# Block encoder on one core: Strassen-Winograd products of the feed-forward chained in the PSUM banks

## The chip, the cores and the metric

The kernel runs on one core of a Trainium2 chip. The metric is the device time of one execution in microseconds (us), from runs of the whole program; TensorE's matmul queue is PE, its weight loads are PEld, VectorE is DVE, ScalarE is ACT, GpSimd is POOL, and SP is the queue that issues all the transfers of the kernel.

## The reference, cut to what matters

One encoder layer on 1024 tokens of width 1024: attention and a pooling mixer with an output projection, and then a SwiGLU feed-forward of inner width 2816, all in float32.

```python
h = rmsnorm(x, norm2_g)
x = x + (jax.nn.silu(h @ w_gate) * (h @ w_up)) @ w_down
```

## The kernel before, in words

Every float32 operand is split into a high part in fp32r and the rest ("hi" and "lo"), and every product of two 128-row pieces is three matmuls with 512 columns: hi·hi, hi·lo, lo·hi (`PASSES`). A split costs two instructions: a copy or cast for hi (ACT, DVE or POOL), and one subtraction for lo (DVE or POOL, `combine`, line 337).

The front half (projections, pooling, attention, output projection, up to about 440 us) is not touched. What follows is the feed-forward:

- Four plain tiles each for the first gate and up block (`plain_tile`), while the sums T1 to T4 of the normed activations are made (`sums_of`).
- Twenty blocks, ten of gate and ten of up in turn (`block`). A block makes 256 inner channels for all 1024 tokens as a 2 x 2 product in the Strassen-Winograd form: seven products of 12 matmuls. Its left operands are A11, A12, A22 and the sums S1 = A21 + A22, S2 = S1 - A11, S3 = A11 - A21, S4 = A12 - S2 of the weights. The right ones are B11, B21, B22 and T1 to T4. The products are P1 = A11·B11, P2 = A12·B21, P3 = S4·B22, P4 = A22·T4, P5 = S1·T1, P6 = S2·T2, P7 = S3·T3, and with U2 = P1 + P6 and U3 = U2 + P7 the four parts of the result are C11 = P1 + P2, C12 = U2 + P5 + P3, C21 = U3 - P4, C22 = U3 + P5.
- After every second pair of gate and up a down stage (`down_sums`, five in all): the same form with activations on the left and rows of `w_down` on the right, for two pairs at once (index i = 0, 1) and four row tiles t. Each of the seven names is 2 x 4 x 3 = 24 matmuls into four banks, 168 in a stage. `drain` adds the banks to the residual rows `qp`.
- A last, plain down product (`down`) and the stores.

In `block` before, every product has a bank of its own (`any_bank`, eight banks in two pools). DVE or ACT reads each bank once or more: P1 is copied to `u` on ACT, P6, P5, P7 are added to sums `u` and `x` in SBUF on DVE (`added`, line 1297), and `emit` adds a bank to a sum on DVE (lines 1252 and 1269), applies SiLU on ACT (line 1258), or multiplies on DVE (line 1272). In `drain` a bank goes straight into `qp` (line 1384) or through sums: two of four rows keep U2 in SBUF and add it to `qp` from there on DVE or POOL, the other two keep it in the bank and take P6 and P7 in through a copy `temp` on ACT.

The order of the work is made by a planner (`Flow`) when the program is built: every vector instruction has a cost, jobs have ranks from the deadline that TensorE sets them, and each engine gets one fixed queue. `flow.tensor(cost, ...)` moves the planner's clock on by the cost of three matmuls. `K["down"]` holds a surcharge per product name that sends work from DVE to POOL in the down stage. Operands are prepared up to two products ahead (`AHEAD = 2`) in three `ring` buffers; right operands of the down stage go to three `raw` buffers or to `wk` slots.

Of the kernel before, what the change touches and what calls it, by code (L numbers as in the profile page):

```python
# [18 lines left out]
P = 128  # L19
# [23 lines left out]
NSLOT = 33  # L43
# [9 lines left out]
    "down": [1.35, 1.05, 1.25, 1.25, 0.75, 1.65, 0.95], "wide": 2,  # L53
# [219 lines left out]
def block_kernel(  # L273
# [667 lines left out]
    def open_silu():  # L941
        late["half"] = sb(ctx, "half", bufs=8, side="right")
        late["sums"] = work()
# [120 lines left out]
    DOWN = ("A11", "A12", "S1", "S2", "S3", "S4", "A22")  # L1064
    STEADY = ("A11", "S1", "A12", "S2", "S3", "S4", "A22")
# [3 lines left out]
    for b in range(len(blocks)):  # L1069
        stream += [(b, name) for name in (FIRST if b < 2 else STEADY)]  # L1070
        if b % 4 == 3:
            stream += [((b // 2 - 1, b // 2), name, i) for name in DOWN for i in range(2)]
# [66 lines left out]
    def product(bank_, w, name, start=True, stop=True):  # L1139
        for i in range(PARTS):  # L1140
            x, job = moving(name, i)
            flow.tensor(0.649, w[1], job)
            for j, (a, b) in enumerate(PASSES):
                nc.tensor.matmul(bank_, w[0][:, a, i], x[:, b], start=(start and i == 0 and j == 0), stop=(stop and i == PARTS - 1 and j == 2))  # L1144

    silu, gated, g_raw, g_job, users = {}, {}, {}, {}, []
# [19 lines left out]
    def sums(p, name):  # L1166
# [22 lines left out]
        elif name == "S4":  # L1189
            job = go(a(0, 1), a(0, 1), a(1, 0), ALU.subtract, made["S2"], made["split A12"])  # L1190
# [7 lines left out]
        elif name == "T4":  # L1198
            job = go(b(1, 0), b(0, 1), b(1, 0), ALU.subtract, made["T2"], made["split B21"])
# [5 lines left out]
    def make_pair(p, name):  # L1205
# [3 lines left out]
        left = {"A11": (0, 0), "S1": (1, 0), "A12": (0, 1), "S2": (1, 0), "S3": (0, 0), "S4": (0, 1), "A22": (1, 1)}[name]  # L1209
# [8 lines left out]
        if name == "S4" or (name == "A22" and p % 2 == 1):  # L1218
            y = pieces()
            waits_r += [made["split T3"], made["T4"]]  # L1220
# [10 lines left out]
        if name == "S2":  # L1231
            sums(p, "S3")
            sums(p, "S4")
            sums(p, "T4")
            sums(p, "T3")
        return (x, jl), (y, jr)

    def emit(b, q, psum, name, plus, *waits):

        kind, p = blocks[b]  # L1240
        f, h = 2 * p + int(q[0]) - 1, int(q[1]) - 1
        if kind == "g":
            s = late["half"].tile([P, HALF], F32, tag="half", name="silu")

            def first():
                yield list(waits)
                if plus is None:
                    yield act(512)
                    nc.scalar.activation(s, psum, AF.Silu)
                else:  # L1250
                    yield dve(512)
# [414 lines left out]
```

## Time and profile before

| | |
|---|---|
| runs (3), median | 1125.41 us (1124.94 to 1126.28) |
| profiled execution, its own time | 1121.88 us |
| its span, first to last instruction | 1120.1 us |
| mean granted TensorE clock, share of 2.4 GHz | 0.994 |
| PE busy | 1074.5 us, 96% of the span |
| DVE, POOL, ACT busy | 871.0, 555.6, 455.8 us |

The time of an execution is its span and 1.8 us around it. Busy time of an engine holds what an instruction waited inside it; idle time in front of an instruction is given with what ended it. Starts are in us from the start of the span.

### The profile page before, as it was taken

How to read it: one execution, taken by the hardware profiler on the slowest of the kernel's cores; microseconds unless marked ns; L12 is line 12 of the kernel's file. 1: busy time of each engine (PE TensorE's matmuls, PEld its weight loads, DVE VectorE, ACT ScalarE, POOL GpSimd, SP SyncE). 2: the span in 40 equal slices, each digit the busy share in tenths (PEclk: the TensorE clock that was granted, in tenths of full speed). 3: DMA queues.
4: the chain of work that ended last, by engine and by line, in shares of the span. 5: the costliest groups of instructions: out<-in, count | busy, mean ns of one | idle time of the engine just before them, and what ended most of it. 6: DMA issues, size and time to landing. Idle time of an engine off the chain costs nothing.

```text
span 1120.1 us, 14036 instructions
## 1 busy us (share of the span) xinstructions
PE 1074.5 (96%) x5114; PEld 877.6 (78%) x5114; DVE 871.0 (78%) x1371; ACT 455.8 (41%) x810; POOL 555.6 (50%) x454
## 2 busy tenths in 40 slices
PE   6989988999999999999999999999899999999998
PEld 5967876888888888878778877888688867887787
DVE  7886699976676776787997689767976698668985
ACT  6513367666676654622332233222422232223420
POOL 3182575533334214664863388236843486238820
PEclk9999999999999999999999999999999999999999
DMA  7111111000000101030123002210122012200113
GB/s 264 53 36 60 37 57 38 19 20 13 16 20 10 30 29 50 27 119 14 36 66 106 19 0 95 61 71 1 38 94 94 1 38 77 94 19 4 53 57 151
DMA packets 42565, 58.49 MB, mean 52 GB/s; under 512 B 4224, under 2 KB 32768, under 8 KB 42496
## 3 DMA queue, kind: packets, MB, share of 16 engines
q1 hardware_dynamic: 42496, 57.59, 15.9%
q8 instruction: 40, 0.66, 0.2%
q14 instruction: 29, 0.24, 0.1%
HBM read 53.39 MB, written 4.19 MB: 51 GB/s over the span
## 4 chain that ended last, share of the span: by engine, by line
PE 72%; DVE 14%; POOL 4%; issue 3%; ACT 1%; DMA 0%; DVEq 0%; ACTq 0%; POOLq 0%
PE b L1144 35%; PE b L1417 8%; PE b L890 8%; PE b L853 5%; PE b L840 5%; PE b L810 5%; DVE wk L337 2%; POOL wk L337 2%; DVE silu L337 2%; DVE qp L1384 2%; PE b L1369 2%; PE b L583 2%; DVE ring L337 1%; DVE wk L1297 1%; DVE qp L337 1%
## 5 line engine op out<-in xcount | busy, mean ns | idle before, releaser
L1144 PE MATMUL b<-wk,ring 128*128 128x512 f32 x1872 | 427.1, 389 | 1.8 <-DVE ring L324 1.8
L1144 PEld LDWEIGHTS b<-wk,ring 128*128 128x128 f32 x1872 | 350.8, 188 | 76.6 <-DVE ring L324 2.3
L1417 PE MATMUL b<-raw,ring 128*128 128x512 f32 x660 | 158.6, 394 | 8.8 <-POOL raw L337 3.6
L1417 PEld LDWEIGHTS b<-raw,ring 128*128 128x128 f32 x660 | 121.9, 188 | 43.8 <-POOL raw L337 8.4
L337 POOL TENSOR_TENSOR ring<-raw,ring 128x512 fp32r<-128x512 f32 x59 | 78.1, 1324 | 150.4 <-ACT ring L322 123.6
L829 POOL TENSOR_SCALAR wk<-wk,rsm 128x1024 f32<-128x1024 f32 x64 | 74.7, 1174 | 141.4 <-ACT wk L821 76.9
L322 ACT ACTIVATE ring<-raw 128x512 fp32r<-128x512 f32 x85 | 52.9, 630 | 206.7 <-PE b L1144 92.4
L331 DVE TENSOR_TENSOR wk<-b,wk 128x512 fp32r<-128x512 f32 (+1 forms) x160 | 101.5, 658 | 37.7 <-ACT wk L322 37.6
L322 ACT ACTIVATE wk<-b 128x512 fp32r<-128x512 f32 (+1 forms) x160 | 90.1, 576 | 80.3 <-PE b L840 60.4
L1384 DVE TENSOR_TENSOR qp<-qp,b 128x512 f32<-128x512 f32 (+1 forms) x167 | 105.6, 675 | 12.4 <-PE b L1369 9.0
L337 DVE TENSOR_TENSOR ring<-raw,ring 128x512 fp32r<-128x512 f32 x91 | 78.4, 867 | 44.3 <-POOL ring L326 22.2
L890 PE MATMUL b<-wk 128*128 128x512 f32 x384 | 102.3, 396 | 0.0
L337 POOL TENSOR_TENSOR wk<-wk 128x512 f32<-128x512 f32 (+3 forms) x55 | 78.4, 1439 | 26.1 <-ACT wk L322 14.8
L810 PE MATMUL b<-kT,wk 128*128 128x512 f32 x256 | 89.1, 430 | 0.0
L853 PE MATMUL b<-wk,vv 128*128 128x512 f32 x256 | 81.8, 398 | 4.7 <-DVE wk L331 4.5
L322 ACT ACTIVATE ring<-silu 128x512 fp32r<-128x512 f32 x65 | 40.9, 629 | 109.6 <-PE b L1417 32.3
L890 PEld LDWEIGHTS b<-wk 128*128 128x128 f32 x384 | 70.8, 188 | 15.2
L819 DVE TENSOR_REDUCE nm<-b 128x1 f32<-128x1024 f32 x64 | 77.9, 1217 | 3.8 <-PE b L810 2.6
L821 ACT ACTIVATE wk<-b,nm 128x1024 f32<-128x1024 f32 x64 | 71.4, 1115 | 18.9 <-DVE nm L819 18.5
L337 POOL TENSOR_TENSOR ring<-silu,ring 128x512 fp32r<-128x512 f32 x45 | 60.5, 1344 | 36.4 <-ACT ring L322 36.4
L840 PE MATMUL b<-ident,wk 128*128 128x128 f32 x512 | 76.7, 272 | 0.7 <-POOL wk L829 0.7
L840 PEld LDWEIGHTS b<-ident,wk 128*128 128x128 f32 x512 | 63.5, 140 | 17.5 <-POOL wk L829 0.9
(145 smaller groups left out, 1590.8 us busy)
## 6 DMA issues: line engine op xcount, KB each, us to landing
raw<-in_w_gate_dram SPq DMA_DIRECT2D x22, 512.0 KB, 3.7
raw<-in_w_up_dram SPq DMA_DIRECT2D x22, 512.0 KB, 3.8
wk<-in_w_down_dram SPq DMA_DIRECT2D x20, 512.0 KB, 5.2
raw<-in_w_in_dram SPq DMA_DIRECT2D x10, 512.0 KB, 3.8
qp<-in_x_dram SPq DMA_DIRECT2D x8, 512.0 KB, 8.0
raw<-in_w_out_dram SPq DMA_DIRECT2D x8, 512.0 KB, 3.4
out_dram<-qp SPq DMA_DIRECT2D x15, 256.0 KB, 2.0
raw<-in_x_dram SPq DMA_DIRECT2D x14, 256.0 KB, 2.7
```

The source lines that it names most:

```text
L322: nc.scalar.activation(hi, src, AF.Copy)
L331: nc.vector.tensor_tensor(lo, src, hi.bitcast(F32), op=ALU.subtract)
L337: (nc.gpsimd if way[0] == "G" else nc.vector).tensor_tensor(dst, a, b, op=op)
L810: nc.tensor.matmul(s[:, c * 512:(c + 1) * 512], qT[t][0][:, h * P:(h + 1) * P], kT[:, kv, b, c * 512:(c + 1) * 512], start=(b == 0), stop= ...
L819: nc.vector.tensor_reduce(nm, s, axis=AX, op=ALU.max, negate=True)
L829: nc.gpsimd.tensor_scalar(pe, pe, rs, 1.0, op0=ALU.mult, op1=ALU.mult)
L840: nc.tensor.transpose(pt[:, j * P:(j + 1) * P], pe[:, c * P:(c + 1) * P], ident)
L853: nc.tensor.matmul(po[t, kv], vt, ps[:, b], start=(c == 0 and b == 0), stop=(c == NT - 1 and b == 1))
L890: nc.tensor.matmul(self.py, mix[self.t][a][:, k, :], wo[k][b][:, self.cs], start=(self.i == 0 and i == 0), stop=(self.i == NK - 1 and i == 2))
L1144: nc.tensor.matmul(bank_, w[0][:, a, i], x[:, b], start=(start and i == 0 and j == 0), stop=(stop and i == PARTS - 1 and j == 2))
L1384: nc.vector.tensor_tensor(dst, dst, src, op=op)
L1417: nc.tensor.matmul(banks[t][0], x[:, a, t * P:(t + 1) * P], y[:, b], start=(i == 0 and j == 0), stop=(i == 1 and j == 2))
```

## The change

Three banks serve the seven products of a block. P1, P6, P7 and P4 follow each other in one bank, so that it holds P1, then U2, then U3, then C21 (the sign of T4 is turned round for this). P5 and P3 follow each other in a second bank, P2 has a third. Each state that is needed is read between two products; before TensorE adds the next product to a bank it waits for the reading, and a whole product in another bank lies between. The order of the names becomes A11, S1, S2, S4, S3, A12, A22. The down stage does the same with four banks for A11, S2, S3, A22, four for S1, S4, and four again for A12, and every state goes straight from the bank into its block of `qp`: `drain` is gone. Three `wk` slots more are paid for by a smaller descriptor scratch. The planner's cost of three matmuls goes from 0.649 or 0.648 to 0.68, and `K["down"]` becomes 0.9 throughout.

```diff
-NSLOT = 33
+NSLOT = 36
+SCRATCH = 4096
...
-    "down": [1.35, 1.05, 1.25, 1.25, 0.75, 1.65, 0.95], "wide": 2,
+    "down": [0.9] * 7, "wide": 2,
...
-    DOWN = ("A11", "A12", "S1", "S2", "S3", "S4", "A22")
-    STEADY = ("A11", "S1", "A12", "S2", "S3", "S4", "A22")
+    STEADY = ("A11", "S1", "S2", "S4", "S3", "A12", "A22")
...
-            flow.tensor(0.649, w[1], job)
+            flow.tensor(0.68, w[1], job, *(waits if i == 0 else ()))
...
-            job = go(a(0, 1), a(0, 1), a(1, 0), ALU.subtract, made["S2"], made["split A12"])
+            job = go(a(1, 0), a(0, 1), a(1, 0), ALU.subtract, made["S3"], made["split S2"], g_job[2 * p + 1, 0])
...
-            job = go(b(1, 0), b(0, 1), b(1, 0), ALU.subtract, made["T2"], made["split B21"])
+            job = go(b(1, 0), b(1, 0), b(0, 1), ALU.subtract, made["T2"], made["split B21"])
...
+        py, held = any_bank()
+        product(py, operand("A11"), "B11")
+        j = copied(u, py, *of_u)
+        pz, held_z = any_bank()
+        product(pz, operand("S1"), "T1")
+        jz = copied(v, pz, *of_v)
+        product(py, operand("S2"), "T2", start=False, more=True, waits=[j])
+        jx = copied(x, py, *of_x)
+        product(pz, operand("S4"), "B22", start=False, more=True, waits=[jz])
...
+        product(py, operand("S3"), "T3", start=False, more=True, waits=[jx])
...
+        pw, held_w = any_bank()
+        product(pw, operand("A12"), "B21")
...
+        product(py, operand("A22"), "T4", start=False, more=True, waits=[j2])
...
+        BANKS = {"S2": "A11", "S4": "S1", "S3": "A11", "A22": "A11"}
+        INTO = {"A11": (0, 0), "S1": (NR, 1), "S2": (0, 1), "S4": (0, 1), "S3": (NR, 1), "A12": (0, 0), "A22": (NR, 0)}
+        for k, name in enumerate(STEADY):
...
+                    waits = [read[own, t]] if i == 0 and own != name else []
+                    flow.tensor(0.68, jx, jy, *waits)
...
+                        row, c = INTO[name]
+                        job = read[own, t] = into(row + t, c, psum)
```

Where instructions stand now. First ACT, in a gate block and the up block behind it (`b1`, `b3` are banks; `silu`, `wk_4535`, `wk_4536` take the states; `ring` is a left operand's hi). Before:

```order
L1290 ACTIVATE wk_4535<-b3_5600 128x512
L322 ACTIVATE ring_5625<-raw_5451 128x512
L322 ACTIVATE ring_5666<-raw_5451 128x512
L1258 ACTIVATE silu_5664<-silu_5664 128x512
L322 ACTIVATE ring_5708<-raw_5601 128x512
L1258 ACTIVATE silu_5704<-silu_5704 128x512
L1258 ACTIVATE silu_5726<-silu_5726 128x512
L322 ACTIVATE ring_5728<-raw_5601 128x512
L1258 ACTIVATE silu_5745<-silu_5745 128x512
L1290 ACTIVATE wk_4535<-b1_5746 128x512
```

And now:

```order
L1310 ACTIVATE silu_5556<-b3_5580 128x512
L1310 ACTIVATE silu_5557<-b3_5558 128x512
L1258 ACTIVATE silu_5557<-silu_5557 128x512
L1258 ACTIVATE silu_5556<-silu_5556 128x512
L323 ACTIVATE ring_5673<-raw_5559 128x512
L1258 ACTIVATE silu_5555<-silu_5555 128x512
L1258 ACTIVATE silu_5690<-b3_5558 128x512
L323 ACTIVATE ring_5694<-raw_5559 128x512
L1310 ACTIVATE wk_4535<-b1_5691 128x512
L1310 ACTIVATE wk_4535<-b1_5712 128x512
L323 ACTIVATE ring_5730<-raw_5559 128x512
L1310 ACTIVATE wk_4536<-b1_5691 128x512
```

Three bank copies per block stand on ACT where one stood (the first of this gate block is the row ahead of these), and the last SiLU of a gate block reads its bank.

Second, POOL at the start of a steady down stage (`silu` holds the gated values and their sums, `wk` rows of `w_down` and their sums, `ring` and `raw` the split left and right operands). Before:

```order
L326 TENSOR_SCALAR ring_7045<-silu_6636 128x512
L326 TENSOR_SCALAR raw_7046<-wk_6576 128x512
L337 TENSOR_TENSOR ring_7045<-silu_6636,ring_7045 128x512
L337 TENSOR_TENSOR raw_7046<-wk_6576,raw_7046 128x512
L337 TENSOR_TENSOR silu_6891<-silu_6891,silu_6869 128x512
L337 TENSOR_TENSOR ring_7091<-silu_6617,ring_7091 128x512
L337 TENSOR_TENSOR raw_7092<-wk_6536,raw_7092 128x512
L337 TENSOR_TENSOR raw_7117<-wk_6812,raw_7117 128x512
L337 TENSOR_TENSOR silu_6617<-silu_6617,silu_6555 128x512
L337 TENSOR_TENSOR wk_6536<-wk_6576,wk_6536 128x512
```

And now:

```order
L327 TENSOR_SCALAR ring_6909<-silu_6385 128x512
L327 TENSOR_SCALAR raw_6910<-wk_6426 128x512
L338 TENSOR_TENSOR ring_6909<-silu_6385,ring_6909 128x512
L338 TENSOR_TENSOR raw_6910<-wk_6426,raw_6910 128x512
L338 TENSOR_TENSOR wk_6426<-wk_6482,wk_6426 128x512
L338 TENSOR_TENSOR silu_6385<-silu_6385,silu_6383 128x512
L338 TENSOR_TENSOR wk_6689<-wk_6744,wk_6689 128x512
L338 TENSOR_TENSOR ring_6953<-silu_6385,ring_6953 128x512
L338 TENSOR_TENSOR silu_6647<-silu_6647,silu_6645 128x512
L338 TENSOR_TENSOR ring_6978<-silu_6647,ring_6978 128x512
L338 TENSOR_TENSOR wk_7025<-wk_6744,wk_7025 128x512
```

The two split operands in front are A12's before and S1's now, and the sums T2 (`wk_6426`) and S2 (`silu_6385`) of the first pair stand four and three places earlier. From the first to the last down matmul POOL's queue holds 18 subtractions and additions and 6 TENSOR_SCALAR; the queue of DVE holds 22 instructions of line 338 there, and 28 bank readings belong to the stage.

Third, DVE in the same stage, from the splits of S2's right operand on. Before, behind the readings of three products:

```order
L337 TENSOR_TENSOR silu_6555<-silu_6595,silu_6617 128x512
L337 TENSOR_TENSOR ring_7136<-silu_6617,ring_7136 128x512
L337 TENSOR_TENSOR wk_6536<-wk_6536 128x512
L1384 TENSOR_TENSOR qp_84<-qp_84,b3_7138 128x512 x2
L1384 TENSOR_TENSOR qp_84<-qp_84,b3_7143 128x512 x2
L1384 TENSOR_TENSOR qp_84<-qp_84,b1_7150 128x512 x2
L337 TENSOR_TENSOR ring_7161<-silu_6891,ring_7161 128x512
L1384 TENSOR_TENSOR qp_84<-qp_84,b3_7154 128x512 x2
```

And now, behind the readings of one product:

```order
L338 TENSOR_TENSOR wk_6426<-wk_6426 128x512
L338 TENSOR_TENSOR raw_6954<-wk_6426,raw_6954 128x512
L338 TENSOR_TENSOR silu_6383<-silu_6384,silu_6385 128x512
L1414 TENSOR_TENSOR qp_84<-qp_84,b1_6955 128x512
L1414 TENSOR_TENSOR qp_84<-qp_84,b3_6960 128x512
L338 TENSOR_TENSOR raw_6979<-wk_6689,raw_6979 128x512
L338 TENSOR_TENSOR silu_6385<-silu_6518,silu_6385 128x512
L1414 TENSOR_TENSOR qp_84<-qp_84,b1_6966 128x512
L338 TENSOR_TENSOR wk_7001<-wk_6482,wk_7001 128x512
L338 TENSOR_TENSOR silu_6645<-silu_6646,silu_6647 128x512
L338 TENSOR_TENSOR ring_7000<-silu_6385,ring_7000 128x512
L338 TENSOR_TENSOR silu_6647<-silu_6780,silu_6647 128x512
```

A bank of S1 was read twice and is read once; the operands of S2 (`raw_6954`, `raw_6979`) and of S4 (`wk_7001`, `ring_7000`) and the sums S3 and S4 stand between its four readings.

## Rows read from the trace of the kernel before

**Rows 1.** Page, busy time, share of the span and instructions by engine.
```profile
PE 1074.5 (96%) x5114; PEld 877.6 (78%) x5114; DVE 871.0 (78%) x1371; ACT 455.8 (41%) x810; POOL 555.6 (50%) x454
```
**Rows 2.** Chain that ended last, in time: start, us, engine, tile, count; down stages one, four, five.
```profile
529.72 9.53 PE b L1417 x42
...
574.00 76.16 PE b L1144 x336
...
890.96 9.54 PE b L1417 x42
...
936.78 76.16 PE b L1144 x336
...
1012.94 9.53 PE b L1417 x42
...
1057.17 38.08 PE b L1144 x168
```
**Rows 3.** Windows, two pairs of blocks and the down stage behind: busy us by engine, instructions.
```profile
573.84:650.00 76.16, 76.16 (x337) 63.06 (x336) 54.53 (x81) 18.91 (x31) 27.95 (x23) 1.00 0.20 66
650.00:694.23 44.23, 40.43 (x170) 30.95 (x168) 40.72 (x52) 17.00 (x29) 38.97 (x29) 1.00 0.11 30
```
**Rows 4.** Timeline of PE, second down stage: start, us, instructions, idle before and what ended it.
```profile
667.42 1.45 PE L1417 MATMUL b<-raw,ring 128*128 128x512 f32 x5 [0.71 <-POOL raw L337]
...
672.17 8.41 PE L1417 MATMUL b<-raw,ring 128*128 128x512 f32 x34 [0.41 <-DVE ring L337]
...
682.95 0.97 PE L1417 MATMUL b<-wk,ring 128*128 128x512 f32 x3 [0.56 <-DVE wk L1297]
685.24 3.71 PE L1417 MATMUL b<-wk,ring 128*128 128x512 f32 x15 [1.33 <-DVE wk L1297]
```
**Rows 5.** Groups of DVE by form, 650.00 to 694.23: busy, mean ns, idle before.
```profile
L1384 DVE TENSOR_TENSOR qp<-qp,b 128x512 f32<-128x512 f32 x24 | 15.1, 678 | 0.5 <-PE b L1417 0.4
...
L1297 DVE TENSOR_TENSOR b<-b,temp 128x512 f32<-128x512 f32 x4 | 2.8, 690 | 0.1
L1297 DVE TENSOR_TENSOR wk<-b,wk 128x512 f32<-128x512 f32 x4 | 2.6, 680 | 0.1
...
L1272 DVE TENSOR_TENSOR silu<-b,silu 128x512 f32<-128x512 f32 x2 | 1.4, 687 | 0.0
...
L1269 DVE TENSOR_TENSOR b<-b,wk 128x512 f32<-128x512 f32 x1 | 0.7, 699 | 0.1
```
**Rows 6.** Groups of POOL by form, the same stretch, the two TENSOR_SCALAR.
```profile
L326 POOL TENSOR_SCALAR ring<-silu 128x512 fp32r<-128x512 f32 x1 | 0.6, 625 | 2.2 <-PE b L1144 2.2
L326 POOL TENSOR_SCALAR raw<-wk 128x512 fp32r<-128x512 f32 x1 | 0.6, 620 | 0.0
```
**Rows 7.** Timeline of POOL, then of DVE, in the same stage.
```profile
651.43 1.29 POOL L337 TENSOR_TENSOR ring<-silu,ring 128x512 fp32r<-128x512 f32 x1
652.68 1.29 POOL L337 TENSOR_TENSOR raw<-wk,raw 128x512 fp32r<-128x512 f32 x1
653.93 1.74 POOL L337 TENSOR_TENSOR silu<-silu 128x512 f32<-128x512 f32 x1
...
654.44 1.77 DVE L337 TENSOR_TENSOR raw<-wk,raw 128x512 fp32r<-128x512 f32 x1
...
667.84 3.66 DVE L1384 TENSOR_TENSOR qp<-qp,b 128x512 f32<-128x512 f32 x6
```
**Rows 8.** Groups of ACT by form, 573.84 to 694.23: hi copies and bank copies.
```profile
L322 ACT ACTIVATE ring<-raw 128x512 fp32r<-128x512 f32 x16 | 10.0, 631 | 42.4 <-PE b L1144 18.7 <-DVE raw L337 11.0 <-POOL raw L337 9.3
...
L1290 ACT ACTIVATE temp<-b 128x512 f32<-128x512 f32 x4 | 2.4, 594 | 3.7 <-DVE b L1297 3.7
```
**Rows 9.** Timelines of PE and DVE where the first gate block of this form begins.
```profile
493.78 35.94 PE L1144 MATMUL b<-wk,ring 128*128 128x512 f32 x156 [1.83 <-DVE ring L324]
...
492.24 1.48 DVE L324 CAST ring<-raw 128x512 fp32r<-128x512 f32 x1
494.37 0.42 DVE L324 CAST ring<-raw 128x512 fp32r<-128x512 f32 x1
```

More of the change, by code (lines that the diff above doesn't have):

```diff
@@ new lines, in place, with half, emit_gate, gen @@
+    def place(b, q):
+        return 2 * blocks[b][1] + int(q[0]) - 1, int(q[1]) - 1
+    def half(name, dt=F32):
+        return late["half"].tile([P, HALF], dt, tag="half", name=name)
+    def emit_gate(q, src, name, part, *waits):
+        s = half("silu") if part is None else part
+        def gen():
+            yield list(waits)
+            if part is not None:
+                yield dve(512)
+                nc.vector.tensor_tensor(s, src, s, op=ALU.add)
+        def last(job):
+            yield [job]
+            yield act(512)
+            nc.scalar.activation(s, src if part is None else s, AF.Silu)
+        job = flow.add(gen())
+        end = flow.add(last(job))
+        silu[q] = s, end
+        if name is not None:
+            flow.hold(name, end if part is None else job)
+        return job
@@ new lines, in emit_up, with whole, kept, times @@
+    def emit_up(b, q, src, name, part, *waits):
+        f, h = place(b, q)
+        s, sjob = silu[q]
+        def whole():
+            yield list(waits)
+            if part is not None:
+                yield dve(512)
+                nc.vector.tensor_tensor(src, src, part, op=ALU.add)
+            yield [sjob]
+            yield dve(512)
+            nc.vector.tensor_tensor(s, src, s, op=ALU.mult)
+        def kept():
+            yield list(waits)
+            yield dve(512)
+            nc.vector.tensor_tensor(part, src, part, op=ALU.add)
+        def times(job):
+            yield [job, sjob]
+            yield from combine(512, s, part, s, ALU.mult)
+        if name is None:
+            job = flow.add(kept())
+            end = flow.add(times(job))
+        else:
+            job = end = flow.add(whole())
+            flow.hold(name, job)
+        g_raw[f, h], g_job[f, h] = s, end
+        if b + 1 == len(blocks):
+            if not gated:
+                hi, lo = (lambda t: (t[:, 0], t[:, 1]))(pieces())
+            else:
+                hi, lo = (half("g", F32R) for _ in range(2))
+            gated[f, h] = hi, lo
+            g_job[f, h] = flow.add(chain(split(hi, lo, s, 512, both=True), end))
+        return job, end
@@ L1316, in block @@
-        j2 = added(u, u, b6, e11)
-        flow.hold(n6, j2)
-        j3 = added(x, u, b5, j2, *users)
-        flow.hold(n5, j3)
-        b7, n7 = bank_of("S3", "T3")
-        j4 = added(u, u, b7, j3)
-        e22 = emit(b, "22", b7, n7, x, j4)
-        b3, n3 = bank_of("S4", "B22")
-        e12 = emit(b, "12", b3, n3, x, j3)
-        b4, n4 = bank_of("A22", "T4")
-        users[:] = [e22, e12, emit(b, "21", b4, n4, u, j4)]
+        gate = blocks[b][0] == "g"
+        u, v, x = [half("silu") for _ in range(3)] if gate else late["sums"]
```

164 lines of the change are left out of this document (48 added, 116 removed).

## The prediction

> **What bounds the kernel now.** First the page: PE is busy for 96% of the span [rows 1], so only what makes PE wait can be won, and the question is where that is. The chain of waits in time order answers it. In the twenty blocks it runs through PE alone: 336 matmuls in 76.16 us [rows 2], which is 0.2267 us each and 2.72 us for a product of 12, without a gap. In a down stage it leaves PE. The 168 matmuls would take 168 x 0.2267 = 38.08 us, just what the last two blocks need for as many [rows 2]; but the first stage takes from 529.72 to 574.00, 44.28 us, and the last from 1012.94 to 1057.17, 44.23 us [rows 2]; the second is as long [rows 3], and so is the third. The fourth takes 45.82 us, from 890.96 to 936.78 [rows 2]. So a stage loses 6.15 to 6.2 us, and 7.7 once: about 32 us in all. That is all the change can find in the stages.
>
> Why a stage is late is read from the windows. In the stage DVE is busy for 40.72 and POOL for 38.97 of 44.23 us; in the blocks for 54.53 and 27.95 of 76.16 us [rows 3]. Busy hides waiting here. POOL's subtractions start 1.25 us apart when nothing disturbs them, and then one takes 1.74 us; DVE's next to it takes 1.77 us [rows 7], while six DVE additions that read a bank run at 0.61 us each beside a busy POOL [rows 7]. So a DVE instruction with both inputs in SBUF and one of POOL exclude each other: 1.77 is hardly less than 1.25 + 0.6, and each waits for the other's end. Of DVE's 52 instructions in the stage [rows 3] 24 + 4 + 4 + 2 + 1 = 35 read a bank [rows 5], so 17 have both inputs in SBUF. Of POOL's 29 [rows 3] two are the short kind [rows 6], so 27 are the long one. If they run one at a time, that is 17 x 0.61 + 27 x 1.25 = 44.1 us, and the stage lasts 44.23: in it the two engines' common turn is taken throughout. PE's waits in the stage [rows 4] name POOL's and DVE's operands and DVE's sums in turn, as they would if whatever comes next is late.
>
> **The change, part by part.** *Down stage.* Bank readings fall to 28 (seven names, four row tiles), the copies `temp` and the additions from SBUF into `qp` go. By the order of the changed program the two engines have 22 DVE instructions with both inputs in SBUF and 18 long ones of POOL between the first and the last down matmul, in each of the five stages. The common turn is then taken for 22 x 0.61 + 18 x 1.25 = 35.9 us, under PE's 38.08. DVE itself needs (22 + 28) x 0.61 = 30.5 us. So the bound passes back to PE on the average; what is left is lateness in places, because the queues are fixed and the spare is only 2.2 us.
>
> I follow the queues by hand for it, with t = 0 at the first down matmul, POOL at 1.25, DVE at 0.61, a TENSOR_SCALAR at 0.62 [rows 6], a hi copy on ACT at 0.63 [rows 8], and the two engines alternating when both want the turn. S1's left operand needs the buffer that the last product of the block gives back at 0; POOL then does two hi (to 1.35), two lo, T2 and S2 of the first pair and T2 of the second, with two DVE splits in between, to 8.8. DVE's T3 follows, POOL's lo of S2, and DVE's lo of T2 ends at 11.25. PE wants it with the second matmul of S2, 49 x 0.2267 = 11.11: with 0.1 for the semaphore **0.24 us** late. S2 of the second pair is on POOL until 12.5, its hi on ACT until 13.15, and DVE's lo of the second T2, behind two readings of S1's banks and POOL's lo, ends at 15.1 where 14.07 was wanted: **1.13** more. S4's operands need the sum S4, one reading, the lo of B22, the sum S3 and, with POOL's lo of the other B22 in front, end at 19.35, where a PE that is 1.37 late wants them at 18.15: **1.3**. T3's lo on POOL costs S3 **0.3**. From there on (A12, A22, the next gate's operands) everything is 2 to 4 us early by the same count. Sum 2.97 us a stage where 6.15 to 6.2 stand now, so five stages win 5 x 3.2 = **16 us**. Ends: 1.0 us late a stage if DVE gets the turn first in the two large places, 4.5 if it loses it there once more: 25.9 to 8.3 us. I take the middle, since the rows show strict alternation [rows 7]. The 1.6 us by which the fourth stage is longer than the others I leave as they are; no row says whether they return.
>
> A rule bears on how far this can go. In the rows the turn is taken by two kinds of instruction, and no row shows a TENSOR_SCALAR of POOL beside a DVE instruction with two SBUF inputs. The Trainium skill, SBUF — State Buffer, section "Who interferes with whom", says that any GpSimd instruction that reads SBUF excludes such a DVE instruction, and that casts on DVE take the shared ports too. By that rule the six TENSOR_SCALAR count as well, the turn is taken for 35.9 + 6 x 0.62 = 39.6 us, and no order of the queues gets a stage under that, 1.5 us late: it speaks against the first rival below. The cast that took 1.48 us where another took 0.42 [rows 9], with POOL busy in between, agrees with it.
>
> *Blocks.* A block loses four DVE readings and gets two more ACT copies (three for one), 0.59 us each [rows 8]. ACT is busy for 18.91 of 76.16 us in the four blocks of a period [rows 3], so 8 x 0.59 = 4.7 us fit in, and DVE's 16 readings fewer (10 us of 54.53) matter nowhere on PE's chain. New is the wait before S2, S4, S3 and A22: the bank must have been read. The reading starts when the product has ended and has the 2.72 us of the product between; ACT's copy needs 0.59, DVE's addition 0.69 [rows 5], and in the order ACT's instruction ahead of each copy is a hi split that is due earlier. Bounds: nothing where the engine is free, and 0.6 to 1.7 us where it holds one other instruction of ACT or DVE; all of it is less than 2.72. Cost nothing; the cover is that product, and without it each of the four waits would show at about 0.7 us.
>
> *The first block of the form.* It waits 1.83 us now for the cast of S1 [rows 9], since the T sums and their splits keep DVE and POOL at the turn. In the order now the cast goes to ACT, but S1's lo stands behind one more split and one reading, 0.61 to 1.77 and 0.61 us, and S2 follows S1 at once. I take **1 us** more; ends 0 (ACT's hi is earlier by what the lo is later) and 4 (S2 and S4 late too).
>
> *The rest.* The three `wk` slots let right operands of A12 and A22 be split before a `raw` buffer comes free; that is inside the count above. Transfers keep their sizes and queue; the second half of a block's weights is asked for two products earlier and the second row block of w_down one product later, so that on SP it now stands behind that half and its buffer, which S3's split gives back; both are wanted a product or more after that. The last block yields its parts in another order, C21 last as before. Nothing.
>
> Sum: 16 - 1 = 15 us. From the profiled execution's 1121.88 us this leads to about 1107, and as that execution lies 3.5 us under the median, the median goes from 1125.4 to **1110.5 us**.
>
> **The rivals.** *All of the lateness goes.* If the turn is given in the better order each time, 35.9 us hide under PE and five stages win 32 us; with 1 us lost at the start that is 1094. For it: the spare of 2.2 us. Against it: the fixed queues and the four places above.
>
> *The re-entry takes the place of the old wait.* In a stage S1's and A11's banks are eight, all there are, and S4 may not start a row tile before DVE has read S1's bank. The readings stand between operands in DVE's queue; the fourth ends at 20.55 by my count, wanted at 21.0, so 0.5 us is all the room. If DVE runs 2 us later than counted, S2, S4 and S3 each wait for about 2 us, 6 us a stage as before, and the time stays at 1125. For it: PE waits 0.56 and 1.33 us for DVE's sums out of banks now [rows 4]. Against it: a state is read once where two of the seven were read two or three times. The Trainium skill, PSUM — Partial Sum Buffer, section "Summary: rules for kernel authors", advises another bank where one is read while matmuls run, which is what the change gives up; by that advice this rival would be the likely one, and the old waits out of banks agree with it in part.
>
> *Slower: the weights' sums in the blocks.* S1, S2 and S4 are sums of each other, written over the same raw block, and A12 no longer stands between S1 and S2. Split lo of S1, difference, hi, lo of S2 is 1.25 + 0.6 + 0.6 + 0.61 to 1.77 + 0.63 + 1.77 us when POOL and DVE meet in it, against one product's 2.72. If this decides, S2 and S4 are each late by up to 0.7 us, 1.4 in a block, 28 us in twenty, and with the 15 won the time is 1138. The point from which it is slower is 0.75 us a block. Against it: operands are prepared two products ahead, and the turn is free for half of the blocks' time.
>
> **How the numbers follow.** Chances: forecast 0.66, all gone 0.14, re-entry 0.10, slower 0.10. The forecast's own ends are 1125.4 - 25.9 = 1099.5 and 1125.4 - 8.3 + 4 = 1121. The range reaches down to the second case and leaves the other two out: 1093 to 1121. What a measurement of this kernel can tell from no change is 0.2%, 2.25 us. Faster by more takes the forecast and the second case, 0.80; the re-entry rival gives 0.08 within 0.2% and adds 0.02 to slower, 0.12.
>
> **What would show it.** In the timeline of PE a down stage of about 41 us with its gaps in S2 and S4 and hardly any in A12 and A22; the blocks still 76.2 us for 336 matmuls; in the windows of a stage POOL's busy time down from 39 to under 32 us; ACT's three copies per block. Wrong would be: gaps in the blocks, waits of S4 for line 1414 as the main ones, or a stage that is as long as before with POOL far less busy, which would undo the reading of the common turn.

## The result and the profile after

The median went from 1125.70 to 1106.56 us (four runs each; 1105.82 to 1107.57 after), a ratio of 0.983, interval 0.981 to 0.985. The forecast was 1110.5, the range 1093 to 1121. The profiled execution took 1107.57 us.

The page of the changed kernel, busy time by engine, beside [rows 1]: DVE has 88 instructions fewer and POOL 17.

```profile
PE 1070.7 (97%) x5114; PEld 881.4 (80%) x5114; DVE 789.3 (71%) x1283; ACT 427.8 (39%) x765; POOL 523.5 (47%) x437
```

The windows that answer to [rows 3], the pair of blocks and the second down stage (length, then busy us and count of PE, weight loads, DVE, ACT, POOL; granted clock; DMA):

```profile
576.36:652.52 76.16, 76.16 (x338) 63.07 (x336) 40.42 (x64) 19.28 (x33) 27.20 (x23) 1.00 0.18 56
652.52:692.91 40.39, 39.09 (x169) 31.14 (x168) 38.36 (x51) 11.69 (x20) 32.51 (x24) 1.00 0.18 53
```

The blocks are as long as before to the hundredth, with 14 us less of DVE in them. The stage went from 44.23 to 40.39 us; the other four are 40.35 to 40.44. PE's timeline of this stage, in place of [rows 4]:

```profile
652.52 11.55 PE L1452 MATMUL b<-raw,ring 128*128 128x512 f32 x50
664.39 3.11 PE L1452 MATMUL b<-raw,ring 128*128 128x512 f32 x12 [0.32 <-POOL ring L338]
668.48 2.58 PE L1452 MATMUL b<-raw,ring 128*128 128x512 f32 x10 [0.97 <-POOL ring L338]
670.90 5.72 PE L1452 MATMUL b<-wk,ring 128*128 128x512 f32 x24
676.45 5.74 PE L1452 MATMUL b<-raw,ring 128*128 128x512 f32 x24
682.03 11.04 PE L1452 MATMUL b<-wk,ring 128*128 128x512 f32 x48
```

Against 0.2267 us a matmul the second row starts 0.53 late (652.52 + 50 x 0.2267 = 663.86), the third 1.37: two waits of S2 for a lo split on POOL, 1.9 of the 2.3 us that the stage still loses. No wait for a bank reading is left, where the stage of before had those for L1297 in [rows 4] and two for L1384:

```profile
669.16 0.97 PE L1417 MATMUL b<-raw,ring 128*128 128x512 f32 x3 [0.29 <-DVE qp L1384]
670.36 1.41 PE L1417 MATMUL b<-raw,ring 128*128 128x512 f32 x5 [0.23 <-DVE qp L1384]
```

POOL's rows say why the two waits of S2 are left, and DVE's what stood beside them (the last three lines):

```profile
652.85 1.09 POOL L327 TENSOR_SCALAR ring<-silu 128x512 fp32r<-128x512 f32 x1 [1.00 <-PE b L1144]
653.90 1.06 POOL L327 TENSOR_SCALAR raw<-wk 128x512 fp32r<-128x512 f32 x1
...
662.60 1.73 POOL L338 TENSOR_TENSOR ring<-silu,ring 128x512 fp32r<-128x512 f32 x1
...
684.07 0.62 POOL L327 TENSOR_SCALAR ring<-silu 128x512 fp32r<-128x512 f32 x1
...
652.77 0.68 DVE L338 TENSOR_TENSOR ring<-silu,ring 128x512 fp32r<-128x512 f32 x1
653.37 1.10 DVE L338 TENSOR_TENSOR silu<-silu 128x512 f32<-128x512 f32 x1
...
682.87 2.47 DVE L1414 TENSOR_TENSOR qp<-qp,b 128x512 f32<-128x512 f32 x4
```

The two hi copies at the head of the queue take 1.09 and 1.06 us beside DVE instructions with two SBUF inputs, where the one at 684.07 takes 0.62 while DVE reads banks. So a TENSOR_SCALAR takes the common turn too. The row at 662.60 is the split that the first of PE's waits names; it ends at 664.33.

The start was lost more dearly than forecast: 92.39 us from the first plain tile to the first stage, against 88.57 before.

```profile
477.70 20.52 PE L1144 MATMUL b<-wk,ring 128*128 128x512 f32 x82 [2.08 <-DVE ring L338]
499.17 0.73 PE L1144 MATMUL b<-wk,ring 128*128 128x512 f32 x2 [0.95 <-ACT ring L323]
500.86 35.23 PE L1144 MATMUL b<-wk,ring 128*128 128x512 f32 x154 [0.96 <-DVE ring L338]
```

The waits here are 2.2 us longer than the 1.83 us of before [rows 9]. The rest of the 3.8 us is the granted clock: the 82 matmuls of the first row took 20.52 us where 82 x 0.2267 is 18.6, and the window over them has a clock of 0.92 (the figure behind the busy times), where the start of before had 1.00 throughout:

```profile
477.70:498.22 20.52, 20.52 (x82) 16.45 (x82) 16.59 (x18) 2.95 (x5) 16.94 (x12) 0.92 0.38 129
```

### The profile page after: what moved, and what is told of

It is laid out like the page before. It is cut to its first block, busy times and chain, and to the rows that moved or that the text cites. A ratio compares the mean times of both kernels' runs of the same rounds, so it can differ in the third digit from the quotient of the medians.

```text
span 1105.8 us, 13899 instructions
## 1 busy us (share of the span) xinstructions
PE 1070.7 (97%) x5114; PEld 881.4 (80%) x5114; DVE 789.3 (71%) x1283; ACT 427.8 (39%) x765; POOL 523.5 (47%) x437
## 4 chain that ended last, share of the span: by engine, by line
PE 76%; POOL 7%; DVE 6%; issue 2%; ACT 1%; DMA 0%; POOLq 0%; ACTq 0%; DVEq 0%
PE b L1144 36%; PE b L1452 11%; PE b L891 8%; PE b L854 5%; PE b L841 5%; PE b L811 5%; POOL ring L338 2%; PE b L1399 2%; POOL wk L338 2%; PE b L584 2%; DVE wk L338 1%; POOL silu L338 1%; DVE nm L820 1%; POOL raw L338 1%; DVE wk L707 1%
## 5 line engine op out<-in xcount | busy, mean ns | idle before, releaser
L1144 PE MATMUL b<-wk,ring 128*128 128x512 f32 x1872 | 428.7, 391 | 4.0 <-DVE ring L338 3.0
L1144 PEld LDWEIGHTS b<-wk,ring 128*128 128x128 f32 x1872 | 352.0, 188 | 79.2 <-DVE ring L338 3.9
L1452 PE MATMUL b<-raw,ring 128*128 128x512 f32 x480 | 114.8, 395 | 6.5 <-POOL ring L338 6.5
L1452 PEld LDWEIGHTS b<-raw,ring 128*128 128x128 f32 x480 | 88.5, 188 | 31.1 <-POOL ring L338 10.8
L338 POOL TENSOR_TENSOR ring<-raw,ring 128x512 fp32r<-128x512 f32 x48 | 63.1, 1316 | 105.1 <-ACT ring L323 62.6
L338 POOL TENSOR_TENSOR wk<-wk 128x512 f32<-128x512 f32 (+3 forms) x61 | 87.0, 1435 | 34.7 <-ACT wk L323 16.8
L323 ACT ACTIVATE ring<-silu 128x512 fp32r<-128x512 f32 x55 | 34.2, 631 | 131.3 <-PE b L1452 56.7
L1452 PE MATMUL b<-wk,ring 128*128 128x512 f32 x360 | 83.9, 391 | 0.0
L338 POOL TENSOR_TENSOR raw<-raw 128x512 f32<-128x512 f32 x38 | 50.8, 1338 | 68.3 <-DVE ring L338 53.3
L323 ACT ACTIVATE ring<-raw 128x512 fp32r<-128x512 f32 x60 | 37.5, 629 | 110.3 <-DVE raw L338 49.4
L325 DVE CAST ring<-raw 128x512 fp32r<-128x512 f32 x68 | 28.8, 425 | 70.7 <-PE b L1144 44.3
L1452 PEld LDWEIGHTS b<-wk,ring 128*128 128x128 f32 x360 | 67.2, 188 | 15.1 <-DVE ring L338 1.3
```

Source lines behind the costliest of these rows:

```text
L323: nc.scalar.activation(hi, src, AF.Copy)
L338: (nc.gpsimd if way[0] == "G" else nc.vector).tensor_tensor(dst, a, b, op=op)
L1452: nc.tensor.matmul(banks[t][0], x[:, a, t * P:(t + 1) * P], y[:, b], start=(own == name and i == 0 and j == 0), stop=(i == 1 and j == 2), ...
```

## The experiments

The theory on trial: DVE instructions with two SBUF inputs and POOL's exclude each other (the turn), and the sum over the turn sets a stage. Its rivals: the number of bank readings sets it; DVE's queue alone; the planner's cost alone. Ratios are to the kernel before; stage lengths are read from PE's timelines (second stage, if nothing else is said).

**More work at a stage's end.** Both runs add `flow.add(extra(psum, job))` behind each reading of A12 and A22, and differ in what `extra` issues.

```diff
+        nc.gpsimd.tensor_tensor(spare_half, fixed, fixed, op=ALU.add)   # more_pool
+        nc.vector.tensor_tensor(spare_half, psum, fixed, op=ALU.add)    # more_readings
```

> The changed kernel with eight more POOL additions of two SBUF halves in each down stage (after each reading of A12 and A22, into an unused half; nothing reads them). Common turn: the stage's bill rises from 22 x 0.61 + 18 x 1.25 = 35.9 us (39.6 with the six TENSOR_SCALAR) by 8 x 1.25 = 10.0 to 45.9 (49.6), so a stage grows from 40.4 to 45 or more and the time by 23 us or more, to about 1130, although POOL alone would be busy for only 42 us and none of the additions is waited for. Rival (what a stage loses is set by bank readings and the waits for banks): POOL has 8 us of idle time in the stage, the additions fill it, a stage stays at 40.4 and the time within 3 us of 1107.

1112.51 us, ratio 0.988 (0.987 to 0.990). A miss for the theory as I had put it: the stage stayed at 40.38 us. Windows and POOL's timeline:

```profile
653.25:693.63 40.38, 39.02 (x169) 31.14 (x168) 39.32 (x52) 11.24 (x19) 34.48 (x26) 1.00 0.18 53
693.63:770.86 77.23, 76.99 (x337) 62.75 (x336) 42.63 (x63) 21.30 (x36) 31.72 (x27) 1.00 0.17 55
```

```profile
690.20 4.08 POOL L1433 TENSOR_TENSOR wk<-wk 128x512 f32<-128x512 f32 x3
694.24 1.29 POOL L338 TENSOR_TENSOR raw<-raw 128x512 f32<-128x512 f32 x1
695.48 6.86 POOL L1433 TENSOR_TENSOR wk<-wk 128x512 f32<-128x512 f32 x5
```

The extras ran from 690.2 on, behind the last operand that POOL has for the stage, and most in the next block, which they made 1.07 us longer. So the place of the work counts: 10 us more of the turn cost 1.1 us here. As a test of the sum over a stage the run is weak, since less than 3.5 of the 10 us fell into the stage.

> The changed kernel with eight more DVE readings of banks in each down stage (each A12 and A22 bank is read a second time, beside a fixed SBUF half, before it is given back; nothing uses the result). Common turn: a reading of a bank is outside the turn; DVE goes from about 30 to 35 us busy, a stage stays at 40.4 to 41 us and the time within 4 us of 1107. Rival (bank readings set the stage: 35 before, 28 now): with 36 readings a stage goes back towards 44 us, the time to 1120 or more.

1108.21 us, ratio 0.985 (0.983 to 0.986), stage 40.39, blocks 76.41. Eight readings more, as many as the change had taken away and one, cost 0.25 us a period at this place. Their number is not what a stage is long by.

**The same eight additions, from SBUF or from a bank, in the middle of the stage.**

```diff
+                        if name == "A11":
+                            for _ in range(2):
+                                flow.add(extra(psum, job))
...
+        nc.vector.tensor_tensor(spare_half, fixed, fixed, op=ALU.add)   # dve_sbuf
+        nc.vector.tensor_tensor(spare_half, psum, fixed, op=ALU.add)    # dve_bank
```

> The changed kernel with eight more DVE additions in each down stage, two after each reading of an A11 bank, both inputs in SBUF (nothing uses their result). The next run has the same instructions in the same order on every engine, but these eight read a bank as their first input, and S2's matmuls then wait for them as well. Common turn: the eight of this run take the turn from POOL for 8 x 0.61 = 4.9 us, so POOL's subtractions beside them last 1.8 us and the operands of S2, S4 and S3 come later: a stage is 2 to 4.9 us longer than in the next run. Rival (only the length of DVE's queue counts): the two runs agree within 0.5 us a stage.

> As the run before, with a bank as the first input of the eight extra DVE additions. Common turn: they lie outside it, POOL's subtractions beside them stay at 1.25 us, a stage is 40 to 41.5 us, time 1105 to 1112, though S2 has to wait for these readings too. Rival (the length of DVE's queue, or readings of banks as such): 2 us a stage or more above the changed kernel, 1117 or more, like the run before.

1126.93 us, ratio 1.002 (1.001 to 1.003), stage 43.54, and 1127.44 us, ratio 1.002 (1.001 to 1.003), stage 44.11. By length the theory missed: 3 us and more were lost in both, dve_bank is 0.57 us the longer one, and the rival's figures for dve_bank (2 us a stage or more, 1117 or more) came true. Every engine has the same instructions in the same order in both programs, but for the input of the eight. Against the changed kernel the planner also moved other work (two TENSOR_SCALAR of POOL in the stage where six stood), so only the pair compares cleanly. Its rows tell the two apart. dve_sbuf, DVE and then POOL:

```profile
679.75 4.08 DVE L1433 TENSOR_TENSOR wk<-wk 128x512 f32<-128x512 f32 x3
...
686.74 2.13 DVE L1433 TENSOR_TENSOR wk<-wk 128x512 f32<-128x512 f32 x3
```

```profile
679.75 1.83 POOL L338 TENSOR_TENSOR ring<-silu,ring 128x512 fp32r<-128x512 f32 x1
681.55 1.73 POOL L338 TENSOR_TENSOR raw<-wk,raw 128x512 fp32r<-128x512 f32 x1
```

dve_bank, the same instructions in the same places:

```profile
680.34 2.13 DVE L1433 TENSOR_TENSOR wk<-b,wk 128x512 f32<-128x512 f32 x3
```

```profile
680.34 1.27 POOL L338 TENSOR_TENSOR ring<-silu,ring 128x512 fp32r<-128x512 f32 x1
681.57 1.30 POOL L338 TENSOR_TENSOR raw<-wk,raw 128x512 fp32r<-128x512 f32 x1
```

With the bank as one input three DVE additions take 2.13 us and POOL runs at 1.27 and 1.30; with both inputs in SBUF they take 4.08, and POOL 1.83 and 1.73. Where POOL is idle, from 686.2 to 690.2, three from SBUF take 2.13 us as well, so SBUF by itself is not the slower input. That is the turn, with nothing else changed. dve_bank loses its time in another way, in PE's timeline:

```profile
681.89 3.68 PE L1460 MATMUL b<-raw,ring 128*128 128x512 f32 x15 [1.43 <-DVE wk L1433]
686.57 0.97 PE L1460 MATMUL b<-raw,ring 128*128 128x512 f32 x3 [1.00 <-DVE wk L1433]
688.09 1.66 PE L1460 MATMUL b<-raw,ring 128*128 128x512 f32 x6 [0.55 <-DVE wk L1433]
```

S3 may not enter A11's bank before the extra reading is done. This is the re-entry rival of the prediction, made real: the room in front of a re-entry is small in a stage.

**Less work for the turn, in the kernel before and in the changed one.**

```diff
-            u_job[t] = into(t, 1, u[t], in_bank=False, waits=[job])   # no_sbuf_adds
+            u_job[t] = job
-            jobs = [into(r, c, u[t], in_bank=False, waits=[job]) for c in range(2)]
+            jobs = [job]
```

> The kernel before with the six additions per stage from an SBUF half into qp left out (S2 of rows 0 and 1 into column 1, S3 of rows 0 and 1 into both columns; the output lacks these sums). The readings of banks stay 35. Common turn: between the first and last down matmul 17 + 27 long ones become about 15 + 25, the bill falls by 2 x 0.61 + 2 x 1.25 to 3.7 us (the planner moves some splits to POOL instead), a stage comes to 41 to 43 us from 44.25, the time to 1110 to 1120. Rival (bank readings): a stage stays at 44.2 and the time at 1125.

1122.47 us, ratio 0.996 (0.995 to 0.998). The stage is 44.11, 0.12 shorter: a miss for the sum, and the length that the rival had. The timed runs are 0.4% shorter all the same, which no stage or block of the profile shows. It goes with the granted clock of the executions: at a mean clock of 0.992 this kernel took 1122.5 to 1123.6 us, and the kernel before, in executions beside the other experiments, 1122.4 to 1123.1.

```diff
-        way = flow.quicker(act(n), dve_fast(n), pool_scale(n)) if both else act(n)   # hi_off_pool
+        way = (flow.quicker(act(n), dve_fast(n)) if late else flow.quicker(act(n), dve_fast(n), pool_scale(n))) if both else act(n)
```

> The changed kernel with one rule more: in the feed-forward the hi copy of a split may go to ACT or DVE, never to POOL (it had 6 of them in each stage; ACT gets them). What is left in a stage of the changed kernel, 2.3 us, is two waits of S2 for lo splits on POOL, and POOL does two such copies of 1.09 and 1.06 us at the start of the stage, ahead of them in its queue. Theory (POOL's own queue with the common turn makes these operands late): both come 2.1 us earlier, a stage goes from 40.4 to 38.1 to 39.0, five stages win 7 to 11 us, time 1096 to 1101. Rival (what is late sits in DVE's or ACT's part, or the copies move on ACT behind something that is due earlier): the waits only change their releaser, stages stay at 40 to 40.5 and the time at 1104 to 1108.

1110.56 us, ratio 0.988 (0.986 to 0.990): 0.5% slower than the changed kernel, and slower than the rival had it (1104 to 1108, stages of 40 to 40.5); what the rival said of the cause came true. The start fell to 89.82 us, but the stage rose to 41.68. S2's two waits on POOL shrank to small ones (72 matmuls took 17.08 us from 649.81, 0.76 more than 72 x 0.2267), and two on DVE came, in S4 and S3:

```profile
668.27 3.02 PE L1452 MATMUL b<-wk,ring 128*128 128x512 f32 x12 [0.77 <-DVE ring L339]
...
675.27 5.51 PE L1452 MATMUL b<-raw,ring 128*128 128x512 f32 x23 [1.00 <-DVE raw L339]
```

The turn's sum is 21 x 0.61 + 19 x 1.25 = 36.6 us here, 3 less than the changed kernel's 39.6 with its six TENSOR_SCALAR, and the stage is 1.3 longer.

**A replay instead of a sum.** The theory had to be put again: the losses in a stage come from the turn, but through the queues, where one POOL instruction in front of a DVE one (or the other way round) holds back the operand or the reading that is next. I replayed the queues by fixed rules: each engine takes its instructions in the program's order, each starts when the ones it waits for have ended, DVE 0.60 us, POOL 1.25, its TENSOR_SCALAR 0.62, ACT 0.53, a matmul 0.2267, and DVE with two SBUF inputs never beside POOL. Stage lengths, second stage; the last column is the replay without the exclusion. It is a calculation, no run:

```
                     measured   replay   without the turn
before                 44.23     43.9        38.1
changed                40.39     40.2        38.1
more_pool              40.38     40.2        38.1
no_sbuf_adds           44.11     43.9        38.7
hi_off_pool            41.68     41.6        38.1
down_alone             41.34     41.3        38.1
dve_sbuf               43.54     44.7        38.1
dve_bank               44.11     44.1        38.3
cost_alone             47.61     47.4        38.5
```

Eight of nine agree within 0.35 us; dve_sbuf is 1.2 off. Without the exclusion no stage would lose more than 0.6 us, by this calculation not even that of dve_bank, whose readings come late in a queue that the turn holds up. All nine had been measured by then, and the agreement hangs on who goes first when both engines want the turn: a plainer rule, first come first served, gives about 42 us for the changed kernel and 45 or more for dve_sbuf, and still leaves the last column near 38.1. So the table says that the exclusion and the order are enough for losses of this size; it doesn't prove each row. What was forecast by it and measured after are the next two runs.

**A planner that knows the turn.** Added to the changed kernel, in the feed-forward alone:

```diff
+    def opens(self, spec):
+        at = self.free[spec[0]]
+        return max(at, self.turn) if self.shared and len(spec) > 2 else at
...
+        if self.shared and len(best.spec) > 2:
+            self.turn = at + cost
...
-        way = flow.quicker(act(n), dve_fast(n), pool_scale(n)) if both else act(n)
+        way = flow.quicker(act(n), (*dve_fast(n), True), *([] if flow.shared else [(*pool_scale(n), True)])) if both else act(n)
...
-        way = flow.quicker(dve(n), pool(n))
+        way = flow.quicker((*dve(n), True), (*pool(n), True))
...
-    "down": [0.9] * 7, "wide": 2,
+    "down": [0.3] * 7, "wide": 2,
```

> The changed kernel with a planner that knows the common turn: in the feed-forward a DVE instruction with two SBUF inputs and one of POOL are planned one after the other, hi copies go to ACT or DVE, and the surcharge on DVE in a stage is 0.3 instead of 0.9. Between the first and last down matmul DVE then has 34 instructions with two SBUF inputs and 24 readings, POOL 6 long ones and nothing else: turn 34 x 0.61 + 6 x 1.25 = 28.2 us, DVE 58 x 0.61 = 35.4 us. A replay of the engines' queues by hand rules (each engine in the program's order with the program's waits, DVE 0.60 us, POOL 1.25, ACT 0.53, one turn for the two) gives stages of 43.9 for the kernel before, 40.2 for the changed one and 41.6 with the hi copies off POOL (measured 44.2, 40.4, 41.7); for this kernel it gives 38.1, with 6.3 us less before the first stage. Theory (a stage is late only where the turn holds an operand or a reading back in its queue): stages 38.1 to 38.7 with no wait of 0.3 us, start 86 to 88, time 1088 to 1093. Rival (DVE's queue, now the fuller one, makes operands late; or the sum over the turn has no part in it): stages 40 us or more, time 1098 or more.

1088.14 us, ratio 0.969 (0.967 to 0.971): 1.4% under the changed kernel (0.969 / 0.983), the fastest of all. PE's timeline of the first stage and the block behind it, and the windows of the second:

```profile
528.10 16.48 PE L1460 MATMUL b<-raw,ring 128*128 128x512 f32 x72
544.42 5.60 PE L1460 MATMUL b<-wk,ring 128*128 128x512 f32 x24
549.86 5.76 PE L1460 MATMUL b<-raw,ring 128*128 128x512 f32 x24
555.45 11.05 PE L1460 MATMUL b<-wk,ring 128*128 128x512 f32 x48
566.34 76.32 PE L1152 MATMUL b<-wk,ring 128*128 128x512 f32 x336
```

```profile
642.50:680.74 38.24, 38.24 (x170) 31.45 (x168) 36.88 (x60) 14.96 (x26) 7.99 (x6) 1.00 0.19 56
```

All five stages take 38.24 us, PE is busy throughout, and the start takes 85.87 us without a pause. DVE does 60 instructions in 36.88 us, so hardly any of them waits; POOL, which had 24, has 6. Three things went together: the turn in the planner, the hi copies off POOL, and the surcharge of 0.3 in place of 0.9, which alone could send work from POOL to DVE. hi_off_pool shows that the second by itself loses; the other two were not run apart, so how much each of them brings is not shown.

> The kernel before with the planner of the run above (turn, no hi copies on POOL, surcharge 0.3, cost 0.68). Its form has 34 readings and 33 other DVE instructions in a stage, 67 x 0.61 = 40.9 us, and 11 to 15 long ones on POOL. Theory: DVE alone needs more than PE's 38.1, so no such order helps the old form; the replay gives stages of 48 to 50 us, the time is 1140 to 1152. Rival (it is the order that wins, whichever the form): stages 38 to 41 us, time 1092 to 1110.

The same planner in the kernel before: 1151.31 us, ratio 1.025 (1.023 to 1.027). Its edit also set the cost to 0.68 in four places ahead of the feed-forward, where the changed kernel keeps 0.648, and its first plain tile starts at 450.74 us instead of 440.98; so 9.8 us of the loss lie outside the stages, and the ratio doesn't tell what the planner does to them. The stages do: they are 47.27 to 53.48 us long. The windows of the second:

```profile
660.48:710.20 49.72, 42.94 (x170) 32.84 (x169) 45.25 (x70) 18.37 (x32) 17.88 (x12) 0.93 0.09 27
```

DVE is given 70 instructions, 45.25 us, more than the stage's 38.1 of PE; a part of the 49.72 us is the granted clock, 0.93. So in the stages this planner wins nothing without the change's form: DVE has room for POOL's work where it has fewer readings and additions of its own. No other surcharge was tried in the old form. In the start it wins there too, 85.86 us against 88.57.

**The parts of the change.**

```diff
-            flow.tensor(0.649, w[1], job)      # cost_alone; also 0.648 of the down stage
+            flow.tensor(0.68, w[1], job)
```

> The kernel before with one thing of the change alone: the planner's cost of a group of three matmuls is 0.68 instead of 0.649 and 0.648. Common turn: the split of the work between DVE and POOL hardly moves (17 to 20 DVE ones with two SBUF inputs, 24 to 28 long ones and 4 to 7 TENSOR_SCALAR of POOL in a stage; bill 43 to 47 with the latter), so stages stay at 43 to 45 us and the time is 1118 to 1128. Rival (the planner's wrong cost made the order late, and the change of it is what wins): stages near 41 us and about 1110.

1137.83 us, ratio 1.011 (1.009 to 1.012), slower than either side had it; stages 43.90 to 47.61, and 94.71 us to the first stage. The new cost alone is a loss of 12 us.

The next two take one half of the diff each, with the changed cost and buffers: `down_sums` as changed, with its surcharge of 0.9, and `block` as before; and the other way round, with the old surcharges.

> The changed kernel's down stage (one bank for A11, S2, S3, A22, a second for S1, S4; the planner's cost and the buffers as changed) with the blocks of the kernel before. In the kernel before a stage's pauses sum to 6.15 us: about 3.6 of them end with a DVE reading of a bank (qp and wk), 2.4 with an operand. Theory (the gain is the down stage's alone: fewer readings of banks and fewer additions): stages 40 to 41.5 us with no wait for a reading, blocks 76.2, time 1104 to 1112. Rival (the blocks' new order, with T4 made late and S1, S2, S4 as sums of each other, carries half of it): stages 42 us or more, or gaps in the blocks, time 1115 or more.

1114.07 us, ratio 0.991 (0.989 to 0.993); stages 41.31 to 41.43, blocks 76.16, start 94.74. The stages are as the theory had them, the time is 2 us over its range and just under the rival's. One of its two larger waits is for a reading, which the theory excluded (PE's timeline):

```profile
670.78 2.57 PE L1423 MATMUL b<-raw,ring 128*128 128x512 f32 x10 [1.17 <-DVE ring L338]
...
676.08 4.09 PE L1423 MATMUL b<-wk,ring 128*128 128x512 f32 x15 [0.56 <-DVE qp L1385]
```

> The changed kernel's blocks with the down stage of the kernel before (and the changed cost and buffers). Theory: the stages keep the old readings and additions and with them their length, 43.5 to 45.5 us, the blocks show up to 1 us where a stage's work is left over, the time is 1126 to 1138; the blocks' part of the change wins nothing by itself. Rival (the new order of products in the blocks is what relieves the stages): stages 41 to 42 us, time 1115 or less.

1132.21 us, ratio 1.007 (1.005 to 1.010); stages 43.96 to 45.72, blocks up to 77.66. Against the new cost alone (1.011) the down stage's form with its surcharge and the buffers brings 2.0%, the blocks' form 0.4%, whose intervals overlap; the blocks' on top of the down stage's brings 0.8% (0.991 to 0.983), of which 2.4 us lie in the start and 0.95 in each stage.

```diff
+    def product(bank_, w, name, start=True, stop=True, waits=(), more=False, cost=0.68):
...
+            product(py, ready[n], f"B{stream[n][1][2]}{h + 1}", start=i == 0, stop=i == 1, cost=0.649)
```

> The changed kernel with the planner's old cost of 0.649 for the plain tiles ahead of the first block of the form; the blocks and stages keep 0.68. From the first product to the first stage it took 88.6 us in the kernel before and 92.4 in the changed one; with the new cost alone in the old kernel it was 94.7. Theory (that cost moves a split of the first S1 and T1 behind others): 88.6 to 90 us, stages as before at 40.4, time 1102 to 1105. Rival (the order of the form S1, S2 one after the other makes the first S2 late): 92 us and 1106 to 1108.

1102.33 us, ratio 0.982 (0.980 to 0.984), start 88.82, stages 40.37 to 40.43. One wait is left, that of [rows 9] at its old size:

```profile
495.59 36.22 PE L1144 MATMUL b<-wk,ring 128*128 128x512 f32 x156 [1.81 <-DVE ring L325]
```

The clock is 1.00 from 457.36 us to the first stage here. So the start's loss in the changed kernel, the longer waits and the fall of the clock behind the first of them, goes with the planner's cost of the plain tiles, not with the order of the form.

## Why the prediction was right, and where it was not

*Where the time goes.* Right: PE alone bounds the blocks, all that can be won lies in the stages and the start.

*The turn and its sum.* The exclusion is right, shown by the pair of runs with SBUF and bank inputs. The step "in it the two engines' common turn is taken throughout", with 44.1 us beside 44.23, comes near the trace: in 42.5 us of that stage a POOL instruction or a DVE one with two SBUF inputs is in progress. What failed is the use made of it, that the sum sets the length of a stage; that the two figures agreed was chance. Counted the same way, the turn is taken for 40.7 us in no_sbuf_adds and the stage is 0.12 shorter; for 37.4 in dve_bank, whose stage is as long; and for 36.6 in hi_off_pool against 38.4 in the changed kernel, with a stage 1.3 longer. What sets the stage, by the replay, is which operand stands behind whom.

*The stage's gain.* The term 5 x 3.2 = 16 us measured 5 x 3.84 = 19.2, from 2.3 us of lateness in place of 2.97. The hand replay had both waits of S2 nearly by size, 0.24 forecast and 0.53 measured, 1.13 and 1.37, but not by cause: it let DVE's lo of T2 be last, and POOL's lo of S2 was, since the two hi copies ahead of it took 2.1 us where it counted 1.25. That is the point at which the Trainium skill, SBUF — State Buffer, section "Who interferes with whom", was weighed, and its rule that every GpSimd instruction reading SBUF excludes such a DVE instruction holds: 1.09 and 1.06 us against 0.62. The 1.3 us for S4 and the 0.3 for S3 did not come. PE does not pause in S4: its last operand, DVE's lo split at 670.60, ended 18.76 us after the stage's start where 19.35 was counted, and PE, held up in S2, came later. The floor of 39.6 us worked out from that rule is none for the kernel: it holds for one split of the work, and turn_planned, with another split and a sum of 28.2, made 38.24. In the changed kernel's stage the trace has the turn taken for 38.4 us.

*Blocks.* Right: 76.16 us, ACT's third copy and the four re-entries hidden. But the cover is a product of 12 and holds for blocks; dve_bank shows three waits of up to 1.43 us where a re-entry in a stage has one reading more in front.

*The start.* The term of 1 us, with ends at 0 and 4, measured 3.8, inside its ends by luck: 2.2 us of waits and about 1.7 of a lower clock, from a cause that the prediction did not name. It looked at the order of S1 and S2, and plain_649 shows that the changed cost did it. The paragraph that ends in "Nothing" had passed that cost over; in the kernel before it costs 12 us by itself.

*The sum.* 16 - 1 was 15; the two terms measured 19.2 - 3.8 = 15.4. That the sums agree is luck: one term was 3.2 us too small, the other 2.8. The profiled pair differs by 14.3 us, as the fourth stage of before had 1.6 more and the part ahead of the feed-forward came 2.6 later this time. The medians differ by 19.1: before's lies 3.8 above its profiled execution, after's 1.0 below. The step that carried 3.5 us over from one to the other is the 3.9 us by which 1110.5 was too high. The executions of the kernel before differ with the granted clock: the profiled one had 0.994, and those beside the experiments took 1121.7 us at 0.994 and 1126.0 to 1126.3 at 0.989, while the four of the changed kernel had 0.991 or 0.992.

*The rivals.* "All of the lateness goes" did not come with this change, but turn_planned shows that it could. The re-entry and the serial sums did not appear. The re-entry's paragraph held that the change gives up another bank for the matmuls beside a reading; in fact they run in another bank, and those that re-enter wait for the reading. Against the serial sums it held the turn free for half of the blocks' time; the trace of before has it taken for 47 of 76 us, and the blocks kept their length all the same.

## What to carry to other kernels

Don't take the sum of an exclusion for the length of a stage: ask for each late operand who stood ahead of it, and replay the queues with the exclusion in them. A planner that places work on two engines which exclude each other should plan them as one resource; here that, with the surcharge that went along, brought nearly as much again as the change (1.4% and 1.7%). A change of form that frees an engine may show its full worth only after the order is planned anew, and a planner's cost that goes along with a change has to be tried alone.

## What was not expected of the hardware

POOL's TENSOR_SCALAR of 128x512 takes 0.62 us by itself and 1.06 to 1.09 beside DVE instructions with two SBUF inputs (changed kernel), and such DVE instructions alternate one by one with POOL's: three in a row took 4.08 us with the turn contended, 2.13 when they read a bank or when POOL was idle (dve_sbuf, dve_bank).

The granted clock (1.00 is the upper of its two levels, 2.4 GHz; less is a mean with the lower, 1.2) was 1.00 in every stage of the changed kernel and of turn_planned, which lose 2.4 us or less. It was 0.96 in the fourth stage of before, 1.6 us longer than its others, and 0.87 in the longest of before_turn_planned, 53.48 us; in both PE had been pausing for operands and readings. In the start of the changed kernel it fell behind the wait of 2.08 us, and the 82 matmuls after it took 20.52 us in place of 18.6. Other stages with the same pauses kept 1.00, as did the start of before behind a wait of 1.83 us, and no run here tells why.
